# A hybrid attention and state-space block on eight cores: SSM weights kept on chip, projections in 256-column pieces, gated loads, new homes for FFN tiles

## The chip, the cores and the metric

The kernel runs on all 8 cores of one Trainium2 chip, one sequence of the batch on each core, without traffic between cores. The metric is the device time of the slowest core in microseconds (us). The four executions of the kernel before agree within 0.3% (2855.2 to 2864.2 us). Some executions fall into a slow state, in which the cores of one die (0 to 3, or 4 to 7), sometimes of both, show a lower granted TensorE clock and run longer. Verdicts use the fast runs only.

Five names are used throughout. In this kernel TensorE multiplies matrices; VectorE, ScalarE and GpSimd do the element-wise work; SyncE and GpSimd's queue start the transfers. In profile lines they are PE (PEld for its weight loads), DVE, ACT, POOL and SP.

## The reference, cut to what matters

```
xn = RMSNorm(x)                                  # x: 2048 rows x 2048 columns a core
[q|k|v|u] = xn @ W_in                            # 1024 + 256 + 256 + 1024 columns
attn = sliding-window attention (window 128, rotary, 16 heads on 4 key/value heads, sinks)
y    = S5 diagonal complex SSM on u              # 64 groups of 16 channels, 64 states
z    = gelu(y);  ssm = z * sigmoid(z @ W_glu + b)        # the GLU
h    = x + RMSNorm(concat[RMSNorm(attn), RMSNorm(ssm)] @ W_o)
out  = h + RMSNorm(SwiGLU(RMSNorm(h)))           # FFN of width 5632
```

Output within tolerance of the float32 reference; weights and matmul operands are bf16.

## The kernel before

The program is written as a list of operations with buffers, priorities and dependencies. When the kernel is built, a list scheduler in it puts them in order: it simulates all engines with modelled durations and, whenever an engine is free, gives it the ready operation of lowest priority number. So the order in which each engine works is fixed at build time by the model. This is the part of the model that sets when a dependent operation counts as ready:

```python
for r in op.rdeps:
    same = (r.eng == e and not op.dma)
    t = op.fin + (0.0 if same else 0.07)         # hand-over between engines: 0.07 us
```

The stages, with cuts marked. Each SSM block of 8 groups has a preparation that computes its weights, and in the kernel before writes them to DRAM; the SSM reads them back through a ring:

```python
def prep(b):                                     # VectorE, GpSimd, 16 small matmuls
    ...
    P.dma(A1T, A1, transpose=True)
    P.dma(wscr[b, :, 0:1024], A1T)               # to DRAM, with 9 more writes for CL and K
    ...
def ssm_pair(q):                                 # 32 of them
    P.dma(wring[hb_ % 3], wscr[hb_ // 2])        # back from DRAM, every second pair
    ...
```

Attention works on 16 tiles of 128 rows, in four steps a tile. A step is a group of score matmuls, a softmax, a DMA transpose of the probabilities P, and a group of value matmuls:

```python
pb_, pt_ = Pb[j % 2], PT[j % 2]                  # two P buffers
T.matmul(scores) ...                             # 4 matmuls of 256 columns
V.tensor_reduce(max); V.tensor_scalar(...)
A.activation(out=pb_, func=Exp)
G.affine_select(pb_) x2                          # the window's mask
P.dma(pt_, pb_, transpose=True)
T.matmul(values from pt_) ...                    # 8 matmuls of 65 columns
```

The output projection of a tile is four pieces of 512 columns, 16 matmuls each, in two PSUM banks. The loop interleaves tile `tt` with the attention of tile `tt + 2`:

```python
for cb in range(4):
    for c in range(16): T.matmul(ps[:, cb % 2, :], lhsT=..., rhs=Wo[c // 4][...])
    A.activation(out=junk[cb % 2], in_=ps[:, cb % 2, :], func=Square, accum_out=...)
    V.tensor_tensor(out=Ab[:, cs], in0=ps[:, cb % 2, :], in1=gpm[:, cs], op=mult)   # eviction
...
for tt in range(16):
    attention(tt + 2); oproj(tt)
```

The FFN's second pair of weight tiles lies in the memory of W_o, so its first load waits for the last output-projection matmul: `WA = [KVO, 0]`, with `Wo` at 0.

## Time and profile before

The median of the runs is 2857.5 us. The profile's page of the slowest core (core 5) begins with the busy times:

```profile
span 2853.9 us, 31443 instructions; the slowest of 8 cores (2814.7 to 2853.9 us)
PE 2614.6 (92%) x12832; PEld 1201.7 (42%) x12832; DVE 785.6 (28%) x1125; ACT 670.0 (23%) x1294; POOL 621.1 (22%) x621
```

TensorE is busy 92% of the span. No other engine passes 28%, so the question is where TensorE stands idle. The table of windows gives each engine's busy time in a stretch (from:to in us, length, then busy time and number of instructions of each engine, the granted TensorE clock, DMA share, GB/s):

```profile
0.00:50.00 50.00, 12.73 (x80) 8.53 (x81) 26.92 (x48) 34.47 (x45) 10.53 (x12) 1.00 1.03 258
50.00:100.00 50.00, 24.68 (x169) 14.66 (x168) 38.64 (x26) 24.53 (x37) 41.23 (x23) 0.69 0.77 183
0.00:200.00 200.00, 119.48 (x710) 62.23 (x712) 117.58 (x114) 104.88 (x165) 100.77 (x70) 0.86 0.92 191
200.00:500.00 300.00, 285.07 (x1532) 134.88 (x1527) 170.30 (x306) 112.32 (x278) 173.48 (x200) 0.95 0.47 95
500.00:655.00 155.00, 107.06 (x522) 47.69 (x521) 71.14 (x106) 90.36 (x121) 46.24 (x52) 0.78 0.56 118
655.00:1012.00 357.00, 304.15 (x1758) 142.58 (x1757) 223.89 (x332) 192.36 (x381) 126.36 (x122) 0.92 0.79 180
1012.00:2820.00 1808.00, 1798.81 (x8320) 814.35 (x8318) 184.79 (x255) 162.52 (x327) 161.82 (x172) 1.00 0.65 96
```

The FFN (last line) has TensorE busy for 1799 of 1808 us at a granted clock of 1.00. The idle time lies before 1012: 80 us in the first 200, 15, 48 and 53 us in the next three stretches. The view of waits, for TensorE alone, says what released it (total us, times, longest):

```profile
PE ps L430 <- DMA PT.121_163<-Pb.119_161: 28.3, 2, 20.5
PE ps L430 <- DVE xs.36_78 L430: 21.5, 5, 9.7
PE ps L430 <- DVE posf.26_68 L430: 18.1, 1, 18.1
PE ps L430 <- DVE Ab.130_172 L430: 17.8, 7, 3.4
PE ps L430 <- DMA ws.6_48<-w_in: 15.0, 1, 15.0
PE ps L430 <- DMA wgt.138_180<-w_gate: 13.4, 1, 13.4
PE ps L430 <- ACT Pb.119_161 L430: 12.0, 8, 1.6
```

One DMA transpose of P held TensorE for 20.5 us; the normalised rows (`xs`) for 21.5 in sum; the output projection's evictions (`Ab`) for 17.8; the FFN's second gate tile (`wgt.138`) for 13.4.

For comparisons I cut the span of every core at four matmuls: the first SSM matmul, the first GLU matmul, the 160th gate matmul of the FFN (gate and up matmuls counted together; a fixed amount of work behind the output projection), and the end. In each part I take the time with no matmul running as idle, and the clock loss as the sum of (1 minus granted clock) times duration, idle time included. These sums are mine, from the matmul and clock records of the profiled run. All are medians over the eight cores, which end 12 to 13 us before the slowest core.

| kernel before | first SSM matmul | projections end | first GLU matmul | 160th gate matmul | end |
|---|---|---|---|---|---|
| at, us | 195 | 489 | 516 | 1007 | 2841 |
| idle in the part that ends here | 80 | | 25 | 88 | 42 |
| clock loss in it | 24 | | 18 | 51 | 18 |

Because the clock loss counts idle time too, it must not be added to the idle time. Counted only while a matmul runs, it is 13, 11, 33 and 2 us in the four parts.

The part from the first GLU matmul to the 160th gate matmul (489 us as the median of each core's difference) is called the back stretch below.

### The profile page before, as it was taken

The page shows a single profiled execution, that of the slowest core. Times are in us where ns is not written, and L with a number is a line of the kernel's source. Part 1 is how long each engine was busy: PE and PEld are TensorE (multiplying, and loading weights), DVE is VectorE, ACT ScalarE, POOL GpSimd, SP SyncE. Part 2 cuts the span into 40 slices and gives each one's busy share as a digit, 9 for nine tenths or more (in the row PEclk, how much of TensorE's full clock was granted, in tenths as well). Part 3 has the DMA queues.
Part 4 walks back from the last instruction along what each step waited for, and adds up shares of the span by engine and source line. Part 5 has one row for each costly group of instructions (what it writes and reads, how often), then busy time and mean ns, then how long its engine had stood idle before and what let it go on. Part 6 is the DMA issues. An engine that isn't in the chain of part 4 may idle for free.

```text
span 2853.9 us, 31443 instructions; the slowest of 8 cores (2814.7 to 2853.9 us)
## 1 busy us (share of the span) xinstructions
PE 2614.6 (92%) x12832; PEld 1201.7 (42%) x12832; DVE 785.6 (28%) x1125; ACT 670.0 (23%) x1294; POOL 621.1 (22%) x621
## 2 busy tenths in 40 slices
PE   2779999589888989999999999989999999999995
PEld 1434444234444434444444444434444444444442
DVE  6735871176766310001110000012111100000003
ACT  5634531475555410000000000021000000000002
POOL 3544775143444100000001111000000000111102
PEclk9889999689999999999999999999999999999997
DMA  9596362736778896657565666689975665655445
GB/s 247 148 154 119 97 119 52 156 64 179 176 192 177 171 121 74 81 68 89 68 80 77 116 104 106 101 158 231 171 89 72 77 78 71 89 94 77 74 81 206
DMA packets 488636, 335.37 MB, mean 118 GB/s; under 512 B 172720, under 2 KB 457776, under 8 KB 479792
## 3 DMA queue, kind: packets, MB, share of 16 engines
q0 software_dynamic: 252032, 159.46, 42.7%
q1 hardware_dynamic: 236464, 173.91, 23.6%
q8 instruction: 104, 1.70, 0.2%
q14 instruction: 36, 0.29, 0.0%
HBM read 398.26 MB, written 57.80 MB: 160 GB/s over the span
## 4 chain that ended last, share of the span: by engine, by line
PE 83%; DMA 6%; issue 3%; DVE 3%; ACT 3%; SPq 1%; another core or an unknown queue 1%; POOL 0%; ACTq 0%; POOLq 0%; DVEq 0%
PE ps L430 83%; SPq L430 1%; DMA PT.121_163<-Pb.119_161 1%; DMA wup.139_181<-w_up 1%; DMA wgt.138_180<-w_gate 1%; DMA uscr<-ust.68_110 1%; DMA hring.159_201<-hscr 1%; DMA zraw.111_153<-zscr 1%; ACT L427 1%; DVE M1.2_44 L430 1%; DMA PT.122_164<-Pb.120_162 0%; DMA idf.27_69<-ident 0%; ACT xnT.1_43 L430 0%; ACT Pb.119_161 L430 0%
## 5 line engine op out<-in xcount | busy, mean ns | idle before, releaser
L430 PE MATMUL ps<-hnT.134_176,wgt.138_180 128*128 128x512 bf16 x1408 | 312.4, 380 | 13.4 <-DMA wgt.138_180<-w_gate 13.4
L430 PE MATMUL ps<-hnT.134_176,wup.139_181 128*128 128x512 bf16 x1408 | 312.3, 380 | 5.9 <-DMA wup.139_181<-w_up 5.9
L430 PE MATMUL ps<-hnT.134_176,wgt.137_179 128*128 128x512 bf16 x1408 | 311.1, 379 | 2.5 <-DMA wgt.137_179<-w_gate 2.5
L430 PE MATMUL ps<-hnT.134_176,wup.140_182 128*128 128x512 bf16 x1408 | 310.9, 379 | 0.0
L430 PEld LDWEIGHTS ps<-hnT.134_176,wgt.138_180 128*128 128x128 bf16 x1408 | 138.0, 98 | 180.9 <-issue 15.8
L430 PEld LDWEIGHTS ps<-hnT.134_176,wup.139_181 128*128 128x128 bf16 x1408 | 137.8, 98 | 173.6 <-issue 8.3
L430 PEld LDWEIGHTS ps<-hnT.134_176,wgt.137_179 128*128 128x128 bf16 x1408 | 137.8, 98 | 168.8 <-issue 3.0
L430 PEld LDWEIGHTS ps<-hnT.134_176,wup.140_182 128*128 128x128 bf16 x1408 | 138.0, 98 | 165.9
L430 ACT ACTIVATE ps<-ps 128x512 f32<-128x512 f32 x64 | 37.3, 583 | 577.7 <-DVE hf2.156_198 L430 287.3
L430 DVE TENSOR_TENSOR hid.154_196<-ev.150_192,ps 128x512 bf16<-128x512 f32 x44 | 30.3, 688 | 433.0 <-PE ps L430 430.2
L430 DVE TENSOR_TENSOR hid.154_196<-ev.152_194,ps 128x512 bf16<-128x512 f32 x44 | 30.3, 688 | 389.4 <-PE ps L430 389.4
L430 ACT ACTIVATE ev.150_192<-ps 128x512 f32<-128x512 f32 x44 | 26.3, 598 | 419.2 <-PE ps L430 403.5
L430 PE MATMUL ps<-ws.6_48,xnT.1_43 128*128 128x512 bf16 x512 | 118.3, 390 | 6.8 <-ACT v1.5_47 L430 6.8
L430 ACT ACTIVATE ev.152_194<-ps 128x512 f32<-128x512 f32 x44 | 26.3, 598 | 396.4 <-PE ps L430 395.5
L430 POOL DMA_DIRECT2D wgt.138_180<-w_gate x22 | 25.1, 1141 | 410.1 <-PE ps L430 410.1
L430 POOL DMA_DIRECT2D wgt.137_179<-w_gate x22 | 25.3, 1148 | 389.9 <-PE ps L430 389.9
L430 DVE TENSOR_TENSOR hf2.156_198<-ps,gpo.149_191 128x512 f32<-128x512 f32 x32 | 22.1, 691 | 278.1 <-PE ps L430 278.1
L430 PE MATMUL ps<-Wo.125_167,qT.3_45 128*128 128x512 bf16 x256 | 72.6, 410 | 20.6 <-DVE Ab.130_172 L430 17.8
L430 PE MATMUL ps<-xnT.1_43,ws.6_48 128*128 128x512 bf16 x256 | 66.7, 426 | 21.6 <-DMA ws.6_48<-w_in 15.0
L430 PE MATMUL ps<-wdn.145_187,hid.154_196 128*128 128x512 bf16 x352 | 80.0, 379 | 0.8 <-DMA wdn.145_187<-w_down 0.8
L430 PE MATMUL ps<-wdn.147_189,hid.154_196 128*128 128x512 bf16 x352 | 80.1, 379 | 0.0
L430 PE MATMUL ps<-wdn.146_188,hid.154_196 128*128 128x512 bf16 x352 | 80.1, 379 | 0.0
(363 smaller groups left out, 3657.7 us busy)
## 6 DMA issues: line engine op xcount, KB each, us to landing
wgt.137_179<-w_gate POOLq DMA_DIRECT2D x22, 1024.0 KB, 9.3
wup.139_181<-w_up POOLq DMA_DIRECT2D x22, 1024.0 KB, 11.4
wgt.138_180<-w_gate POOLq DMA_DIRECT2D x22, 1024.0 KB, 9.3
wup.140_182<-w_up POOLq DMA_DIRECT2D x22, 1024.0 KB, 11.1
xr.129_171<-x SPq DMA_DIRECT2D x16, 1024.0 KB, 6.2
hscr<-xr.129_171 SPq DMA_DIRECT2D x16, 1024.0 KB, 4.6
hf.155_197<-hscr SPq DMA_DIRECT2D x8, 1024.0 KB, 15.1
hf.155_197<-ffscr SPq DMA_DIRECT2D x8, 1024.0 KB, 16.5
```

What stands on the lines that cost most here:

```text
L427: eng.preload_act_table_set(SET_NAME[op.load])
L430: inst = getattr(eng, m)(*a, **kw)
```

## The change

The intent: take the SSM weights' way through DRAM out of the front, bring the u weights and x tiles forward, fill TensorE's holes between SSM and GLU with projection pieces, and give attention and output projection more room. The diff, cut to its core:

```diff
 # scheduler's model
-        op.nb = nb / (200.0 if tr else 280.0) / 1000.0
+        op.nb = nb / (200.0 if tr else 250.0) / 1000.0
-                t = op.fin + (0.0 if same else 0.07)
+                t = op.fin + (0.0 if same else (PE_SLACK if r.eng == "tensor" else SLACK))
+PE_SLACK = 0.6
+SLACK = 0.2
 # x rows wait for the first u weights
-                P.dma(b[:, :], x[...], wk=[("x", tt)])
+                P.dma(b[:, :], x[...], rk=[("wu", 0), ("wu", 1)] if tt > 3 else ())
 # SSM weights: three slots in SBUF, no wscr
+        A1Ts, CLs, KTs = three slots each
-            P.dma(wscr[b, ...], ...)                       # 10 writes a block, a 2 MB zero fill
+                P.dma(kt[16 * j:16 * j + 16, :, 16 * j:128], Kst[0:16, :, 0:128 - 16 * j])
+            if q % 4 == 3 and q < 20:
+                prep(q // 4 + 3)                           # made just in time, between SSM pairs
 # q, k, v: 512 columns at a time -> 256
-                        T.matmul(ps[:, bk, :], lhsT=xnT[:, c, tsl], rhs=sl[:, c, :], ...)
+                        T.matmul(ps[:, bk, 0:256], lhsT=xnT[:, c, tsl], rhs=w[:, c, :], ...)
+        P.prio = 215.0
+        zconv()                                            # GELU conversion among the q pieces
 # GLU in three PSUM banks; priority 405, between attention tiles 0 (400) and 1 (410)
-                    bk = n % 2
+                    bk = (0, 1, 4)[n % 3]
 # attention: a third P buffer
-        Pb = [AO, AO + 2048]
+        Pb = [AO, AO + 2048, AO + 14 * KB]
-                    pb_, pt_ = Pb[j % 2], PT[j % 2]
+                    pb_, pt_ = Pb[(4 * tt + j) % 3], PT[j % 2]
 # W_o in 16 loads of 1024 columns, other homes
-        hn = sb("hn", SO + 46 * KB, ...);  junk at SO + 50 * KB
+        hn = sb("hn", SO + 48 * KB, ...);  junk at CO + 4096
-        WA = [KVO, 0]
+        WA = [KVO, SO + 32 * KB]                           # FFN weights no longer under W_o
+        hid = 44 separate tiles instead of one block
```

## The prediction

> **What bounds the kernel.** The table of windows splits the profiled core (2854 us): 0-200 normalise x, project half of u; 200-500 SSM and q/k/v; 500-655 GELU conversion, GLU, attention tiles 0-1; 655-1012 output projection with attention; 1012-2854 FFN. TensorE is busy 92% overall, at full clock through the FFN, which hardly changes. The gain lies before 1012: there TensorE is busy 816 us, granted clock 0.63 to 1.00. The view of waits names holes: normalised tiles from VectorE 31 us, "posf" 18 (really first loads), u weights 15, a DMA transpose of P 20.5, z tiles 10.6, and 13.4 for an FFN weight at 1000. The chain of waits also crosses 30 us of SyncE's queue at 167-197.
>
> **What the change does.**
> 1. SSM weights skip DRAM: a 2 MB zero fill (36.8 us to land), 80 small writes and 16 ring loads go. SyncE's queue, which delayed the u writes and the first SSM matmul (199.7), clears. Five of eight preparations (VectorE 6 x 1.1 us, GpSimd 6 x 1.7 us each) move into the SSM stage.
> 2. x tiles 4-15 wait for the first u weights, which should land near 45 us, not 70; last x transpose at 105-120, not 143. First SSM matmul at 150-170: about 40 us won.
> 3. q/k/v in 256 columns: 1536 matmuls for 768. Sets of four 256-column matmuls here start 110 ns apart, 512-column ones 217. [...] So weight loads (98 ns) stay hidden: 169 us for 166. Rotary costs more: GpSimd 2 x 0.57 + 0.72 us per piece, just over its 16 matmuls' 1.76 us; the last two pieces give the add to VectorE.
> 4. z conversion moves among the q pieces: 30 us of nearly idle TensorE (500-531) goes. From SSM start to the end of projection I sum 45 + 169 + 63 + 7 = 284 us of TensorE, with about 250 us of VectorE and 260 of GpSimd beside it: all near full. I take 310 us; before took 330 including conversion.
> 5. GLU and attention 0-1: three PSUM banks, weights early, W_o partly earlier. W_o still collides with the first transposes; 105 us for 124.
> 6. Output projection: third P buffer, more slack in the order: 342 us for 357.
> 7. FFN: second weight slot no longer lies under W_o: the 13 us wait goes.
>
> **Sum (estimate).** 160 + 310 + 105 + 342 + 1830 = about 2750 us, nearly all on the critical path because TensorE is the chain. Range 2705 to 2810. Chances: faster 0.82, same 0.16, slower 0.02.
>
> **What would show it.** First SSM matmul at 150-170 in the timeline; no z wait; projection ending near 470; output projection starting near 575-590; gate-weight waits under 3 us; FFN about 1830; mean clock slightly up.
>
> **What would make it wrong.** (a) VectorE and GpSimd, with preparations too, hold TensorE back[...]. Then the stage takes 340 us, the total 2780 or more. (b) W_o loads stall the first P transposes by 20 us again, as at 535. (c) Gate-up matmuls placed earlier in TensorE's order wait for weights before the last attention tile. (d) Gating delays x more than it helps.

The sum is 160 + 310 + 105 + 342 + 1830 = 2747 us, and the 169 us of step 3 are its 1536 matmuls at the measured 110 ns.

## The result and the profile after

The kernel after is correct. Its median is 2831.1 us over 4 runs (2824.9 to 2995.2, one of them slow). The ratio of fast runs, after to before, is 0.9897, 95% interval 0.9861 to 0.9932: 1% faster, inside the 2% that counts as the same. Ratios are the mean time of one kernel's fast runs over the mean of the other's of the same rounds, so not quite the ratio of the medians. The predicted 2750 us and its range (2705 to 2810) were missed.

The page of the slowest core (core 1), the same two lines:

```profile
span 2823.8 us, 33455 instructions; the slowest of 8 cores (2806.1 to 2823.8 us)
PE 2604.0 (92%) x13600; PEld 1271.9 (45%) x13600; DVE 806.1 (29%) x1189; ACT 668.0 (24%) x1324; POOL 609.7 (22%) x696
```

There are 768 more matmuls, as 768 of 512 columns became 1536 of 256, but busy time is not larger. The windows answer to those of before:

```profile
0.00:50.00 50.00, 7.46 (x64) 6.51 (x64) 29.30 (x49) 31.30 (x41) 12.54 (x14) 0.95 0.93 229
50.00:100.00 50.00, 35.53 (x213) 18.78 (x214) 49.40 (x38) 25.28 (x42) 29.48 (x17) 0.78 0.52 138
0.00:200.00 200.00, 130.54 (x773) 67.79 (x774) 116.98 (x138) 110.25 (x181) 58.55 (x48) 0.89 0.67 151
200.00:500.00 300.00, 280.41 (x2306) 209.59 (x2304) 189.88 (x341) 129.11 (x311) 208.91 (x294) 0.96 0.59 94
500.00:655.00 155.00, 108.20 (x552) 47.84 (x550) 83.71 (x135) 76.56 (x121) 47.31 (x58) 0.85 0.59 108
655.00:1012.00 357.00, 319.42 (x1808) 147.47 (x1808) 217.89 (x314) 187.86 (x371) 120.03 (x120) 0.94 0.84 182
```

In the first 50 us TensorE does less than before (7.5 us of work for 12.7), in the next 50 more, while VectorE is full there (49.4 of 50). And the waits:

```profile
PE ps L430 <- DVE xs.37_79 L430: 28.7, 6, 15.6
PE ps L430 <- DVE negib.16_58 L430: 19.9, 1, 19.9
PE ps L430 <- DMA PT.117_159<-Pb.114_156: 17.4, 1, 17.4
PE ps L430 <- DVE Ab.130_172 L430: 15.4, 5, 6.0
PE ps L430 <- DVE ast.25_67 L430: 12.1, 4, 4.0
PE ps L430 <- DVE ast.26_68 L430: 9.3, 4, 4.0
PE ps L430 <- DMA wgt.137_179<-w_gate: 3.5, 1, 3.5
```

Two waits of before have gone: the u weights are out of the list, and so is the FFN's second gate tile (`wgt.138`, 13.4 us before, at 1012). The gate tile that is left is the first one (`wgt.137`), at 1866 us in the FFN's second half, where it cost 2.5 us before. The first transpose of P still stalls (17.4 for 20.5), the normalised rows still do (28.7 and more), and the reduction of the attention's maximum (`ast`) is new among the large ones. In the stage sums:

| kernel after | first SSM matmul | projections end | first GLU matmul | 160th gate matmul | end |
|---|---|---|---|---|---|
| at, us | 165 | 494 | 495 | 975 | 2812 |
| idle in the part that ends here | 66 | | 20 | 82 | 46 |
| clock loss in it | 14 | | 14 | 45 | 20 |

Over the whole span idle time fell from 239 to 211 us (medians), 28 us. The end moved by 29. The prediction had wanted 107 us. The clock loss with a matmul running is 11, 12, 29 and 2 us in the four parts, some 5 us less than before in sum. Note how little of the front's gain lasts: the first SSM matmul is 30 us earlier, the first GLU matmul 21. One reason is in the count of matmuls before the first SSM matmul: of 512 of the u projection, 352 came before it in the kernel before, 304 after. The missing 48 (12.5 us of TensorE's time by the same records) had only moved behind it.

The back stretch fell from 489 to 480 us. Counting to the end of the output projection instead, and leaving out gate matmuls placed earlier, attention, GLU and output projection took 440 us before and 445 after: nothing was won there. What went is the wait for the FFN's gate tiles, 11.6 us before and 0 after in this part (medians over the cores). All idle time of the part fell by 6 us only (88 to 82), so other idle time in it grew by about 6.

### The profile page after: what moved, and what is told of

It is laid out like the page before. It is cut to its first block, busy times and chain, and to the rows that moved or that the text cites. A ratio compares the mean times of both kernels' runs of the same rounds, so it can differ in the third digit from the quotient of the medians.

```text
span 2823.8 us, 33455 instructions; the slowest of 8 cores (2806.1 to 2823.8 us)
## 1 busy us (share of the span) xinstructions
PE 2604.0 (92%) x13600; PEld 1271.9 (45%) x13600; DVE 806.1 (29%) x1189; ACT 668.0 (24%) x1324; POOL 609.7 (22%) x696
## 4 chain that ended last, share of the span: by engine, by line
PE 80%; DMA 7%; DVE 6%; ACT 3%; issue 2%; POOL 1%; SPq 0%; DVEq 0%; POOLq 0%; ACTq 0%
PE ps L430 80%; DMA wup.139_181<-w_up 1%; DMA qT.3_45<-qr.82_124 1%; DMA PT.117_159<-Pb.114_156 1%; DMA qT.3_45<-qr.81_123 1%; DVE M1.2_44 L430 1%; DMA hring.202_244<-hscr 1%; DVE xs.36_78 L430 1%; DMA xr.129_171<-x 1%; DMA qT.3_45<-qr.84_126 0%; DVE xr.129_171 L430 0%; DMA PT.117_159<-Pb.115_157 0%; DVE ast.25_67 L430 0%; DMA A1T.65_107<-A1.43_85 0%; DVE TT.49_91 L430 0%
## 5 line engine op out<-in xcount | busy, mean ns | idle before, releaser
L430 PEld LDWEIGHTS ps<-hnT.134_176,wup.139_181 128*128 128x128 bf16 x1408 | 138.3, 98 | 173.5 <-issue 8.9
L430 PE MATMUL ps<-wh.8_50,xnT.1_43 128*128 128x256 bf16 x768 | 89.4, 276 | 2.3 <-ACT v1.5_47 L430 2.3
L430 PE MATMUL ps<-wh.9_51,xnT.1_43 128*128 128x256 bf16 x768 | 89.9, 278 | 0.7 <-ACT rr.75_117 L430 0.7
L430 PEld LDWEIGHTS ps<-wh.9_51,xnT.1_43 128*128 128x128 bf16 x768 | 76.0, 100 | 12.8 <-issue 2.9
L430 PEld LDWEIGHTS ps<-wh.8_50,xnT.1_43 128*128 128x128 bf16 x768 | 75.2, 99 | 13.7 <-issue 4.5
L430 PE MATMUL ps<-Wo.121_163,qT.3_45 128*128 128x512 bf16 x128 | 42.6, 418 | 41.9 <-DVE Ab.130_172 L430 15.4
L430 POOL DMA_DIRECT2D wup.139_181<-w_up x22 | 25.2, 1144 | 163.2 <-PE ps L430 163.2
```

Of the source, the lines that this page charges most:

```text
L430: inst = getattr(eng, m)(*a, **kw)
```

## The experiments

The theory at this point was that two stages hold back: at the front, SSM preparations on VectorE between the x tiles; at the back, stalls of the first P transposes and the order of attention. The runs on front and start of attention below, two_p and ffn_alone do or undo single parts to test it; the later ones follow what these showed. Times below carry ratios to the kernel before in the same rounds, and stage times of the profiled run. The kernel before itself had fast runs of mean 2855 to 2874 us from one batch of runs to another (2858 and 2874 on the same chip), so stage times of different batches are not compared below 10 us.

### The front

**prep_late**: the kernel after, with preparations 1 to 7 held back in the scheduler.

```diff
+            P.floor = 124.0 if b else 0.0        # not ready before 124 us of the model
             prep(b)
```

> Edit to the changed kernel: the order keeps the SSM preparations of blocks 1 to 7 off every engine until the last x tile is normalised (in the changed kernel VectorE runs about 5.5 of the 8 preparations between x tiles, 49 of 50 us busy at 50-100, while x tiles 5-7 had landed 11 to 20 us before they were squared). Theory (VectorE full of preparations holds x back): last x transpose ends near 122 instead of 138 (median core), first SSM matmul near 150 instead of 165, total 10 to 15 us shorter than the changed kernel's 2812 (median core). Rival (ScalarE, TensorE order and two xs buffers set the pace, or the work comes back in the SSM stage): last transpose within 4 us of 138, or stage 1 shorter and the SSM stage longer by as much, total within 4 us.

Measured: correct, ratio 0.9892 (0.9859 to 0.9924). VectorE in the window from 50 to 100 us, for 49.40 us in the kernel after:

```profile
50.00:100.00 50.00, 40.06 (x253) 20.80 (x254) 24.52 (x17) 31.60 (x52) 3.54 (x3) 0.93 0.53 165
```

The last x transpose came 9 us earlier (129 for 138), so the preparations did hold the x tiles, for 9 us. The first SSM matmul stayed where it was (166 for 165) and projections ended at 500 for 494. The time was given back before the SSM could use it: the rival holds.

**no_late_prep**: the late preparations are left out; the result is wrong on purpose (relative error 0.08).

```diff
-            if q % 4 == 3 and q < 20:
+            if False:
```

> Wrong result on purpose: blocks 3 to 7 use the weights of the slots' earlier blocks and are not prepared. Theory (the preparations hold TensorE back in the SSM stage): from first SSM matmul to the end of the projections 329 us becomes 305 to 312 (15 us of TensorE's idle time and some of the 10 us lost to a lower clock go, besides 4 us of TensorE's own work), and the last x transpose comes some 8 us earlier; total 25 to 35 us shorter. Rival (the stage is bound by TensorE's own work, 302 us by counting): 329 falls by 4 to 8 us only.

Measured: ratio 0.9882 (0.9787 to 0.9978; an unclear verdict, as one run of 2851.7 widens it). From the first SSM matmul to the end of the projections it took 322 us for 329, as the rival had it. The SSM ended at 345 us instead of 386, but projections at 486 instead of 494: of 41 us, 8 arrived. Projection pieces had been filling TensorE's gaps in the SSM all along, and without the gaps they simply came later. Between 345 and 500 us TensorE is busy for 145.6 of 155 us in the kernel after (first line) and for 138.3 in this run (second line), where the projections end before 500.

```profile
345.00:500.00 155.00, 145.56 (x1267) 121.17 (x1266) 81.36 (x153) 54.59 (x119) 113.66 (x193) 0.97 0.75 106
345.00:500.00 155.00, 138.34 (x1183) 116.17 (x1182) 60.77 (x113) 47.10 (x93) 113.86 (x195) 0.96 0.71 100
```

**early_x** and **no_gate**: rotary tables and SSM parameters held back behind the first x tiles; and the gate on the x rows removed.

```diff
+        P.floor = 60.0                           # early_x: rotary tables; parameters 60, preparations 70 and 124
-    P.dma(b, x[...], rk=[("wu", 0), ("wu", 1)] if tt > 3 else ())
+    P.dma(b, x[...], rk=())                      # no_gate
```

> The changed kernel with rotary tables, SSM parameters and all preparations kept out of the order until the first x tiles are through (in the changed kernel x tiles 1 to 3 had landed 5, 8 and 11 us before ScalarE squared them, because it made sine tables first; TensorE was idle 42 of the first 50 us). Theory (start-up order costs TensorE time that nothing later gives back): first u matmul at 40 to 45 instead of 53, last x transpose near 120, TensorE idle before the first SSM matmul 66 -> 48 to 55, total 8 to 15 us shorter than the changed kernel. Rival (as in the run with late preparations, the time comes back before the SSM starts, since that waits for u's second-half weights and the trip of u through DRAM): idle stays 62 to 68, total within 4 us.

> The changed kernel without the wait of x tiles 4 to 15 for the first u weights; every engine's order is unchanged. Theory (the gate brings the weights early and costs x nothing): u weights land at 50 to 70 instead of 33 and 38, TensorE waits for them some 5 to 15 us, total 0 to 10 us longer than the changed kernel. Rival (the gate holds x back): last x transpose earlier than 138 by over 5 us and total shorter.

Measured: early_x 0.9917 (0.9883 to 0.9951). TensorE did 15.3 us of work in the first 50 us for 7.5, and the first u matmul came at 42, as expected, but waits came back later: last x transpose 137 (near 120 expected), idle time before the first SSM matmul 71 us (above both expectations), first SSM matmul 174 for 165, GLU start 505 for 495. no_gate 0.9887 (0.9863 to 0.9911), last x transpose at 138 and first SSM matmul at 165, both as in the kernel after. The u weights landed at 33 and 46 us (33 and 38 with the gate, 44 and 69 in the kernel before), where 50 to 70 was expected, and the first u matmul came at 54 as with the gate. So the gate neither helps nor hurts, and of the 31 us by which the second load comes earlier than in the kernel before it gives 8. Which other part of the change gives the rest (loads that are gone, or the new split of the weight loads) was not tested.

Together: the front's stages are elastic. Work put earlier or later comes out near the same GLU start, because by then TensorE has the sum of the work to do. The gain that lasts there is 14 us of idle time before the first SSM matmul and 6 after it, which is nearly all of the 21 us at the GLU start. TensorE's busy time up to there is the same (411 us before, 410 after): the 256-column pieces took 173.5 us for 169.4 of the 512-column ones by the same records, and the other matmuls together took some 5 us less.

### Start of the attention

**att_first**: attention tiles 0 and 1 ahead of the GLU. **wo_late**: all W_o loads but the first four halves wait for the first two P transposes.

```diff
-GPRIO = 405.0
+GPRIO = 415.0                                    # att_first
+   P.dma(pt_, pb_, transpose=True, wk=[("pt0", j)] if tt == 0 else ())        # wo_late
+   load_wo: rk += [("pt0", 0), ("pt0", 1)]  unless k < 4 and i == 0
```

> Only the GLU's priority number is changed, 405 to 415, so both early attention tiles come before the GLU as in the kernel before. Theory (the 11 us won in the GLU were borrowed: attention tile 1 ended 131 us after the first GLU matmul, where before it was 63, and two output tiles then wait): GLU ends 5 to 10 us later, the second output tile's matmuls are done 150 to 155 us after the first GLU matmul instead of 168, end of output projection 8 to 15 us earlier. Rival (VectorE's and ScalarE's total work sets this stretch): the end of the output projection within 4 us.

> The last 12 of the 16 W_o loads wait until the first two P transposes of attention tile 0 have landed. Theory (W_o's bulk load stretches that transpose to 25 us and TensorE waits 17 us for it): the wait falls under 4 us, the GLU ends 10 to 15 us earlier, output projection starts no later, total 8 to 15 us shorter. Rival: 12 MB of W_o then land too late (about 600) and TensorE waits for W_o instead, total unchanged or longer.

Measured: att_first 0.9887 (0.9848 to 0.9925). Its profile fell in the slow state of one die, so only the other die is read: attention tile 1 was done 82 us after the first GLU matmul instead of 131, yet the back stretch took 480, the same: the theory fell. wo_late 0.9857 (0.9824 to 0.989), back stretch 476. The stall in the kernel after is this transpose; SyncE's timeline gives its start (us) and the time of the issuing instruction, and the view of its tile the landing (the longest is this one):

```profile
513.07 7.76 SPq L430 DMA_TRANSPOSE PT.117_159<-Pb.114_156  x1
```

```profile
DMA to landing us min/median/max: 2.8/14.1/25.5
```

Issued at 513.1, it landed 25.5 us later, with the W_o loads under way (seven of 512 KB issued from 505 to 515 us); the medians of the P transposes over the whole run are 2.8 to 5.4 us. That the loads stretched it is read from this overlap; no run isolates one transpose against one load. The waits for transposes of P in the window from 490 to 650 us, in the kernel after:

```profile
PE ps L430 <- DMA PT.117_159<-Pb.114_156: 17.4, 1, 17.4
PE ps L430 <- DMA PT.117_159<-Pb.115_157: 6.7, 2, 6.4
```

and with the loads held back:

```profile
PE ps L430 <- DMA PT.118_160<-Pb.114_156: 12.3, 1, 12.3
PE ps L430 <- DMA PT.117_159<-Pb.115_157: 9.1, 1, 9.1
PE ps L430 <- DMA PT.117_159<-Pb.116_158: 4.7, 1, 4.7
PE ps L430 <- DMA PT.117_159<-Pb.114_156: 1.3, 1, 1.3
```

The wait for the first transpose fell from 17.4 to 1.3 us, as the theory had it, but the sum did not fall (24.1 us in the kernel after, 27.4 here, on another core). The loads start once two transposes have landed, and then meet the next two: on this core the first two landed after 2.8 and 2.7 us, with no load under way, the third and fourth after 12.0 and 23.2 us, beside the loads. So the collision named in the prediction (W_o against the first transposes) is seen in both kernels, and this run moved it, for some 4 us, but did not remove it. What removing it is worth stays open. (The loads held back are 12 of 512 KB, 6 MB; the expectation's 12 MB is a slip.) **combo** puts both together:

> The kernel after with two changes tried before singly: attention tiles 0 and 1 ahead of the GLU, and the W_o loads behind their first P transposes. If the two add up: stretch 468 to 475, ratio 0.980 to 0.985. If the stretch is bound by the steady order of the tiles that follow: 475 to 481, ratio 0.985 to 0.990.

Measured: 0.9874 (0.985 to 0.9898), back stretch 471, which is in the first expectation's window (468 to 475), while the ratio is in the rival's. Neither this nor wo_late can be told from the kernel after: their intervals overlap.

### The third P buffer and the homes of tiles

**two_p**: the kernel after with two P buffers again. **ffn_alone**: the kernel before with the FFN homes only (with `hn` and `junk` moved, as the change does).

```diff
-        Pb = [AO, AO + 2048, AO + 14 * KB];  pb_ = Pb[(4 * tt + j) % 3]
+        Pb = [AO, AO + 2048];                pb_ = Pb[j % 2]                  # two_p, on after
-        hn at SO + 46 * KB; junk at SO + 50 * KB; WA = [KVO, 0]; hid one block
+        hn at SO + 48 * KB; junk at CO + 4096; WA = [KVO, SO + 32 * KB]; hid 44 tiles   # ffn_alone, on before
```

> The changed kernel with two P buffers again. My prediction gave the third buffer and the new order some 15 us in the output projection. Theory: without it the stretch from the first GLU matmul to the 160th gate matmul, 480 us in the changed kernel, becomes 488 to 500. Rival (P's buffers limit nothing, TensorE's order and VectorE's chain do): within 4 us of 480.

> The kernel before with one part of the change alone: the second FFN weight slot moved off W_o's space, the hidden tiles in separate homes (hn, junk and the FFN sums moved to make room). Theory (the FFN boundary pays on its own): TensorE's wait for the gate weights at about 1000 us (13.4 on the slowest core before) falls under 4, total 11 to 18 us shorter than the kernel before on the median core, ratio about 0.995. Rival (the boundary's gain comes from something else in the change, such as the earlier end of attention): total within 4 us of before.

Measured: two_p 1.0024 (1.0 to 1.0048), back stretch 521 for 480. Taking back one 2 KB buffer took back the whole gain, two to five times what was expected. And ffn_alone, which should have removed a wait, is slower than before: 1.007 (1.0013 to 1.0127), back stretch 511 for 489. Both surprises had the same face, an output projection at some 24 to 25 us a tile in the middle of the stage (the mean of eleven tiles), for 22 both before and after. So the next runs split them.

**move_only**: the kernel before with nothing but `hn` and `junk` moved. **p3_alone**: the kernel before with nothing but a third P buffer (in free memory at CO + 4096). **p3_ffn**: ffn_alone plus the third buffer.

```diff
-        hn = sb("hn", SO + 46 * KB, ...);  junk = sb("junk", SO + 50 * KB + 1024 * i, ...)
+        hn = sb("hn", SO + 48 * KB, ...);  junk = sb("junk", CO + 4096 + 1024 * i, ...)     # move_only
-        Pb = [AO, AO + 2048];                pb_ = Pb[j % 2]
+        Pb = [AO, AO + 2048, CO + 4096];     pb_ = Pb[(4 * tt + j) % 3]                    # p3_alone
```

> The kernel before with only two homes changed: the row before the FFN transpose and the two scratch tiles of the square, put where the kernel after has them. Built, TensorE's order of output projection and attention is the very same as in the run with the FFN homes (which was slower than before), and not that of before: attention comes in clusters. Theory, the order that the scheduler fell into is what made that run slow: stretch from first GLU matmul to 160th gate matmul 505 to 515 us (before 489), ratio 1.003 to 1.012. Rival, FFN weights that arrive during the output projection made it slow: stretch 487 to 493, ratio 0.998 to 1.002.

> The kernel before with one thing more: a third P buffer for the attention probabilities. Undoing that buffer in the kernel after cost 41 us between the first GLU matmul and the 160th gate matmul (480 to 521). Theory A, the third buffer is the gain and stands alone: this stretch falls from 489 to 470 to 480 us, ratio to before 0.992 to 0.997. Theory B, the third buffer alone would bring the whole 1%: ratio 0.990 or below. Rival C, the buffer only mends an order of the output projection that other parts of the change had spoilt: stretch 485 to 492, ratio 0.998 to 1.002.

> The run with the FFN homes alone, plus the third P buffer; SSM, projections, GLU and the scheduler's margins are all as before. Theory, the SSM ring, the 256-column pieces, the gates and the GLU changes net to nothing and the back half holds the gain: stretch 475 to 482, ratio 0.986 to 0.992, like the kernel after (0.990). Rival, the front half holds about half of the gain (the SSM ended 22 us earlier after, at 386 instead of 408, the GLU started 21 us earlier): ratio 0.995 to 1.000, with the GLU starting at 514 to 520 as before.

Measured: move_only 1.0071 (1.0031 to 1.011), back stretch 518. The stretch is 3 us beyond the theory's window, the ratio in it. The FFN homes are not the cause; the new homes of `hn` and `junk` are. They compute nothing different. But TensorE's order as built is another one, and by the matmul records it is the very order of ffn_alone, which had the same ratio (1.007). In the same way no_gate has the order of the kernel after, and its ratio. In these lines a dot is half a piece of the output projection (8 matmuls), s a group of scores, v a group of value products, from the middle of the stage:

```
before       vs..vss....vsv....vsvs...s.vs.v...s.vs..vs.vsv..v
move_only    v..ss..v.s.vsv.v...svs...vs.sv..v..ss..v.s.vsv.v.
after        ss....vvss....vvs.s...vsv....vss.v..s.svv..vs..s.
two_p        ...vs.vsv..v..ss...v.svsv..v..ss...v.svsv..v..ss.
p3_alone     .vsv..v..ss.v.s..svv..v..ss.v.s..svsv...v.s.vs...
```

The waits of TensorE in the window from 655 to 955 us, first three lines in move_only, where evictions alone hold it for 28.5 us:

```profile
PE ps L430 <- DVE Ab.130_172 L430: 28.5, 6, 5.5
PE ps L430 <- DVE ast.23_65 L430: 15.9, 5, 3.3
PE ps L430 <- DMA PT.122_164<-Pb.120_162: 8.7, 11, 2.0
```

and in p3_alone, where the largest entry is 8.1:

```profile
PE ps L430 <- ACT Pb.121_163 L430: 8.1, 6, 2.7
PE ps L430 <- DVE Ab.131_173 L430: 5.4, 3, 2.9
PE ps L430 <- ACT Pb.119_161 L430: 4.2, 3, 2.6
```

p3_alone came out as theory A had it: 0.9957 (0.9918 to 0.9996), back stretch 477. So the third buffer is worth 12 us in the order of the kernel before and 41 us in that of the kernel after: it has no price of its own. p3_ffn: 0.9939 (0.9905 to 0.9972), back stretch 482, GLU start 523. The stretch is in the theory's window; the ratio is between the two expectations and a little nearer to the rival's: about 0.6% comes with third buffer and FFN homes, which would leave 0.4% of the change's 1% to the rest, as far as intervals that overlap can tell. The FFN homes took the gate wait from 8 us (p3_alone) to 1 (p3_ffn), and the stretch was no shorter for it (477 and 482).

### The scheduler's margins

**no_slack**: the kernel after with the scheduler's model of before. **slack_only**: the kernel before with the margins and nothing else. **slack_more**: the kernel after with margins of 1.0 and 0.4 us. **tr_model**: the kernel after, a DMA transpose taken to land 3.0 us after its data has moved instead of 1.9.

```diff
-PE_SLACK = 0.6 ; SLACK = 0.2 ; 250 bytes a ns
+PE_SLACK = 0.07; SLACK = 0.07; 280 bytes a ns    # no_slack (slack_only: the reverse, on before)
+PE_SLACK = 1.0 ; SLACK = 0.4                     # slack_more
-                    op.fin = hw_free + 1.9
+                    op.fin = hw_free + (3.0 if op.calls[0][2].get('transpose') else 1.9)      # tr_model
```

> The kernel after with the scheduler's model put back (0.07 us for every hand-over instead of 0.6 from TensorE and 0.2 from the others; 280 bytes a ns instead of 250). Built, TensorE's order in the output projection turns into a regular pattern of one attention step between pieces. Theory, the time per output tile is set by the order: the regular pattern with three P buffers is at least as good, stretch 465 to 480, ratio 0.984 to 0.990. Rival, the margins are what makes the order fit the chip: stretch 490 to 515, ratio 0.995 to 1.003.

> The kernel before with the scheduler's margins alone (0.6 us after TensorE, 0.2 after the others, 250 bytes a ns); no tile, buffer or load is changed, only the order. Undoing the margins in the kernel after took away its whole gain (1.0005). Theory M, the margins by themselves are the net gain: stretch from the first GLU matmul to the 160th gate matmul 470 to 481 us (before 489), or projections end 10 us or more earlier than 489 to 496; ratio 0.986 to 0.994. Rival, margins pay only with the third P buffer and the new projections: stretch 485 to 510 and projections as before, ratio 0.997 to 1.008.

> The kernel after with larger margins (1.0 and 0.4 us for 0.6 and 0.2). If the order is good because hand-overs are charged what they really take, and they take still more than 0.6: stretch 465 to 477 and ratio 0.982 to 0.988. If each setting only draws another order: anything from 480 to 515, ratio 0.990 to 1.004.

> The kernel after, where the scheduler takes 3.0 us instead of 1.9 for the landing of a DMA transpose (the trace shows medians of 2.8 to 5.4 us from issue to landing for the P transposes). Built, the order in the output projection becomes a regular one, value products and scores in turn. Theory, a model nearer to the chip gives an order with fewer waits: stretch 465 to 477, ratio 0.982 to 0.988. Rival, it only draws another order: 480 to 515, ratio 0.990 to 1.004.

Measured:

- no_slack: 1.0005 (0.9969 to 1.0041). The SSM ended at 374 us, 12 earlier than in the kernel after; projections ended at 513, 19 later; back stretch 501. The rival holds: without the margins none of the gain is left, although SSM ring, 256-column pieces, third buffer and FFN homes are all in. Nothing but the engines' order differs from the kernel after, so here the order alone costs 1%.
- slack_only: 0.9961 (0.9917 to 1.0005), back stretch 483. Neither expectation's ratio is excluded; the margins alone are worth about 0.4% (0 to 0.8), not the whole. The back stretch is in neither window.
- slack_more: 0.9927 (0.9885 to 0.9969), back stretch 490. The first SSM matmul (159) and the GLU start (491) were the earliest of all correct runs here, and the back stretch gave it away: another draw.
- tr_model: five of its six runs, the profiled one among them, were in the slow state, so there is no ratio; the one fast run took 2873.6 us, above the 2855 of the kernel before. On the undisturbed die the back stretch took 528 us, the worst of all. My premise was also mistaken: the model adds 1.5 us of issue and 1.3 us of transfer, so it had a P transpose land 4.7 us after issue already, inside the measured medians of 2.8 to 5.4, and my edit made it 5.8. What the run shows is only that a constant changed by 1.1 us draws an order 48 us worse.

The orders as built, in the same signs as above; each repeats itself tile by tile:

```
slack_only   v..ss.v.s.v.sv..v..ss.v.s.v.sv..v..ss.v.s.v.sv..v
no_slack     ..ssv....vss.v.v..ssv....vss.v.v..ssv....vss.v.v.
slack_more   .s.v..ssv.v.v..s.s.v..ssv.v.v..s.s.v..ssv.v.v..s.
tr_model     .vs..v.vs....vss.vs..v.vs....vss.vs..v.vs....vss.
```

### Evictions and GLU banks

From the 128th output-projection matmul on, I summed TensorE's idle time by the kind of matmul that followed it, a core:

| run | before values | before scores | before output projection | sum | back stretch |
|---|---|---|---|---|---|
| p3_alone | 6 | 11 | 10 | 28 | 477 |
| after | 3 | 5 | 26 | 34 | 480 |
| before | 7 | 11 | 20 | 37 | 489 |
| slack_only | 10 | 0 | 35 | 44 | 483 |
| no_slack | 8 | 24 | 22 | 55 | 501 |
| two_p | 16 | 2 | 39 | 57 | 521 |
| move_only | 17 | 4 | 45 | 66 | 518 |
| tr_model (one die) | 10 | 25 | 36 | 72 | 528 |

The back stretch follows the sum of these waits roughly (slack_only is better than its sum, two_p worse). In the kernel after, waits at the softmax fell (18 to 8), and waits at the output projection's banks rose (20 to 26). It is not shown that the one caused the other: in p3_alone the third buffer lowered the waits at the banks (20 to 10). **evict_first** lets evictions go first; **glu_two** takes the GLU back to two PSUM banks.

```diff
+                P.prio = 495.0 + 10 * tt         # evict_first: before square and eviction; 515 again after them
-                    bk = (0, 1, 4)[n % 3]
+                    bk = n % 2                   # glu_two; sums in bank 7, scores of tiles 0 and 1 double-buffered
```

> The kernel after, where the output projection's evictions (ScalarE's square and VectorE's product of a finished bank) go before attention's steps in the scheduler's choice. From the 128th output-projection matmul on, TensorE of the kernel after stands idle about 34 us a core in these stages, 26 of it just before output-projection matmuls. Theory, banks wait for evictions that queue behind attention's work: idle before output-projection matmuls at or under 15 us, stretch from the first GLU matmul to the 160th gate matmul 466 to 476, ratio 0.982 to 0.988. Rival, the order is only drawn anew; built, it is one of pairs (value product and next scores together), like the run with the longer transposes, whose stretch was 528 us: 495 to 530, ratio 0.995 to 1.008.

> The kernel after with the GLU in two PSUM banks instead of three, sums in the attention's bank again, and double-buffered scores for attention tiles 0 and 1, as before. If the third bank made the GLU faster by the 10 to 19 us that the prediction took: last GLU matmul 112 to 120 us after the first (102 in the kernel after, 116 in the kernel before), stretch 486 to 498, ratio 0.992 to 0.997. Rival, the stretch is set by attention and output projection together and the GLU's part comes back: last GLU matmul late or not, stretch 474 to 484, ratio 0.986 to 0.991.

Measured: evict_first 0.9981 (0.9956 to 1.0006), back stretch 521. Idle time before output-projection matmuls rose to 34 us, before scores to 26, and evictions still stand first among the waits from 655 to 955 us:

```profile
PE ps L430 <- DVE Ab.130_172 L430: 31.1, 11, 3.6
PE ps L430 <- ACT Pb.115_157 L430: 8.0, 4, 2.5
```

My theory fell; the order was drawn anew, as the rival had it. glu_two: 0.9875 (0.9846 to 0.9903), last GLU matmul 103 us after the first for 102. The ratio is the rival's, the back stretch of 489 us is in neither window. The third bank did not bring the last GLU matmul forward. (The first output-projection matmul came 127 us after the first GLU matmul here, for 105 in the kernel after.)

No run here beats the kernel after beyond its interval. wo_late (0.9857) and combo (0.9874) have the best ratios.

## Why the prediction was wrong

The waits that the prediction named were mostly there, and most of those it aimed at did shrink. TensorE is the chain (83% of the chain that ended last before, 80% after), its total busy time stayed (2607 us before, 2603 after, by the sum of each matmul's own time), and idle time was the only thing to win. The amount was wrong. Its sum, part by part, with what it took for the kernel before (slowest core) and what the profiles show (medians of the cores):

| term | predicted | it took for before | gain predicted | measured, before to after | gain measured |
|---|---|---|---|---|---|
| to the first SSM matmul | 160 | 200 | 40 | 195 to 165 | 30 |
| SSM and projections, to the GLU | 310 | 330 | 20 | 321 to 330 | -9 |
| GLU, attention, output projection | 105 + 342 = 447 | 124 + 357 = 481 | 34 | 489 to 480 | 9 |
| FFN | 1830 | 1842 | 12 | 1834 to 1837 | -3 |

Two steps failed most: the front up to the GLU start, where 60 us were forecast and 21 came (steps 2 and 4), and the output projection, where 15 were forecast and none came (step 6).

- **Steps 1 and 2** (DRAM way gone, u weights at 45 us, first SSM matmul at 150 to 170): right in place. The u weights landed at 33 and 38 us, the first SSM matmul came at 165. The weights came early mostly for another reason than the one named: without the gate on x they land at 33 and 46 (no_gate). Wrong as a gain: "about 40 us won" took the date of the first SSM matmul for a gain. 30 us came, 12.5 of them were u matmuls moved behind it, and no_late_prep shows that an earlier SSM hardly moves the projections' end (41 us became 8). "Last x transpose at 105-120" failed too: it came at 138; VectorE's preparations account for 9 us of that (prep_late, 129), the rest is open. "Five of eight preparations move into the SSM stage" holds for the program text, not for VectorE's order.
- **Step 3** (256 columns): right. Sets of such matmuls start 109 to 110 ns apart, beside weight loads of 99 to 100 ns each. Predicted 169 us for 166; 173.5 came, for 169.4 before by the same records.
- **Step 4** (projection in 310 us for 330): the conversion did move among the q pieces; the GLU starts 1 us after the last projection, for 27 before. But TensorE was not "nearly idle" there: in the 30 us from 500 to 530 on the slowest core it had been busy 16. And the sum of 284 us of TensorE was too small: by the records TensorE is busy for 310 us in this part (u 46, q/k/v 173.5, SSM 80 where 63 were summed, conversion 7, preparations 4, which were left out). So the 310 that the prediction took for the whole stage was TensorE's busy time alone, and 20 us of idle time came on top: 330. Against the kernel before (busy 296, idle 25) the stage grew, among other things because 10 us of u matmuls had moved into it. For fear (a) of the prediction, that VectorE and GpSimd hold TensorE back, the front shows one overlap: on the slowest core 13 of the 16 normalising products took 2.34 to 2.35 us, and three between 44 and 73 us took 3.3 to 3.5, while GpSimd ran preparations (busy 35.1 of 36 us from 44 to 80). VectorE's own 128x512 products of the preparations took 1.1 to 1.9 us from 47 to 81, and 0.7 from 85 to 105, when GpSimd stood idle. No run isolates the one engine against the other. The three slow products cost some 3 us in sum, and prep_late, which left one of them, won nothing, so it is not what cost the time at the front. In the SSM stage no_late_prep bounds what the later preparations cost: 8 us at the end of the projections.
- **Steps 5 and 6** (105 for 124, 342 for 357): step 5 came as dated, the first output-projection matmul 105 us after the first GLU matmul for 116 before. But attention tile 1 was pushed behind it (done at 131 us for 63), and from there to the 160th gate matmul it took 378 us for 372. So step 6 failed. Between the first GLU matmul and the end of the output projection nothing was won (440 to 445 us). The stall named in fear (b) came again (17.4 us); wo_late moved it to later transposes, for some 4 us. The third buffer and "more slack in the order" were costed as a sure 15 us. The third buffer is worth 12 us (p3_alone) or 41 (two_p), the margins 0.4% (slack_only) or the whole 1% (no_slack), depending on what else is in, as each draws a new order. Two new homes alone, of `hn` and `junk`, cost 0.7% (move_only), and orders of the same work spread the back stretch from 471 to 528 us.
- **Step 7** (13 us for the FFN's tile): right as a wait, 11.6 us before and 0 after. But the prediction took it off the wrong term: it ends at 1012 and so lies inside the 357 us, while it was subtracted from the FFN (1842 to 1830), which had none of it and did not shrink (1834 to 1837). Nor did taking the wait away shorten the back stretch by itself (p3_alone and p3_ffn).

Fears (c) and (d) did not come true: TensorE waited 0 us for gate and up tiles in the back stretch, and no_gate changed nothing.

What stays open: which property of an order makes it good. The sums of waits separate the orders after the fact. Larger charges for hand-overs (slack_more), later transposes (tr_model) and precedence of evictions (evict_first) did not give a better one, and no_slack, tr_model and slack_only all run in regular periods with very different results. That evictions wait because VectorE takes attention steps in clusters is argued from the waits, not shown.

## What to carry to other kernels

Where a list scheduler orders the engines, an edit has two effects: what it does, and the order that it draws. Here runs that differ from the kernel after in the order alone (no_slack, slack_more, evict_first, tr_model) have one stretch anywhere from 480 to 528 us, a spread of 48 us against a whole gain of 29, so single parts have no price of their own, and a gain should be tested by undoing and by adding each part, with the built order compared. Cost a stage by the idle time in it, not by when its first instruction comes: a stage that starts 30 us earlier may only have passed its work on. And list each wait with the window in which it lies before subtracting it.

## Times of the hardware that these runs show

- Matmuls of 512 columns, sustained: the FFN of the kernel before runs 8320 matmuls, nearly all of 512 columns, in 1808 us (1012 to 2820) at a granted clock of 1.00: 217 ns each. Those of 256 columns start 109 to 110 ns apart.
- The granted clock under such a load: in the fast profiled runs of both kernels all eight cores ran the FFN (1012 to 2820 us) with a granted clock of 0.99 to 1.00. In the slow state of one die (tr_model, core 0 from 1400 us on) the windows show 0.81:

```profile
1400.00:1600.00 200.00, 198.67 (x749) 82.87 (x762) 16.52 (x24) 14.33 (x24) 13.70 (x12) 0.81 0.48 63
```

This clock is met in some executions of a program and not in others: in the one fast run of tr_model the mean granted clock was 0.96 on all eight cores. What decides it is not shown.
- A small DMA transpose beside bulk loads: the first P transpose of the kernel after took 25.5 us to land, where the medians of the P transposes are 2.8 to 5.4; in wo_late the first took 2.8 with the loads held back, and the fourth 23.2 beside them.
